# Split activations that begin 28 bytes into their SBUF slots: a one-layer decoder step on one core

## The chip, the core and the metric

The kernel runs on one core of one Trainium2 chip. The metric is the device time of one execution in microseconds, the median of several runs. Lower is better.

## What is computed

One inference step of a one-layer decoder, in float32, for 256 prompt tokens and 8 x 4 sample tokens (288 in all) at a model width of 2,048. Cut to what matters:

```python
mod = silu(c) @ w_ada + b_ada                       # 2048 -> 6 x 2048
h = rms(x, g_mix) * (1 + sc_m) + sh_m
b_gate, c_gate, hc, u, v, ga, gb = split(h @ w_in)  # 2048 -> 9216
ya = b_gate * causal_conv3(c_gate * hc)
yb = gelu(u) * (spatial_mix(rms(gelu(v))) + b_sg)
merged = sigmoid(ga) * (ya @ w_pa) + sigmoid(gb) * (yb @ w_pb)
x = x + gt_m * (merged @ w_out)
h2 = rms(x, g_ffn) * (1 + sc_f) + sh_f
gate, up = split(h2 @ w_ffn_in)                     # 2048 -> 2 x 5632
x = x + gt_f * ((silu(gate) * up) @ w_ffn_out)
return rms(x, g_final), conv state, v rows
```

Every weight is used once, for all 288 tokens.

## The kernel before

Activations stand transposed: 128 features on the partitions, the 288 tokens along the free dimension. A tile of 128 features x 288 tokens of float32 is one **slot** of the pool `slots`, which has 92 of them (`SLOTS`, line 24). Each slot is padded to 298 words (`TU = T + 10`), because some tiles carry ten extra columns beside the 288. In the built program the slots lie 1,216 bytes apart in each partition and every one begins on a multiple of 32 bytes (32 past a multiple of 64).

Float32 products are made from three matmuls on the faster type `float32r`. An operand `a` is split into `hi`, its rounding to `float32r` (a cast on ScalarE), and `lo = a - hi` (a subtraction on VectorE). `triple` (line 227) then issues `hi·hi` (L229), `hi·lo` with the activation's low part (L232) and `lo·hi` with the weight's low part (L234). All of them accumulate in one PSUM bank. The activation is the moving operand, 288 columns wide; the weight tile, 128 x 128, is loaded before each matmul.

Weights are streamed from HBM in blocks (`raw`), ahead of their use through a ring of 7 buffers, and split in pieces of four tiles into the rings `hi` and `lo` (L453 on ScalarE, L459 or L248 on VectorE). These rings are in another pool than the slots. For each output tile of 128 features, `Blk.run` goes over the tiles of the contraction and calls `triple` for each. A sink then takes the result out of PSUM and does the pointwise work. The order of TensorE's work is written out by hand: the adaLN projection (`ada`, L393, on unsplit float32), the input projection, the two branches, the output projection, and the feed-forward in four quarters.

The split activations are made in these places: `split` (L299 to L304; for `ya`, `yb`, `mg` and `act`), `modulate` (hi at L316, lo at L326; for `h1` and `h2`) and `make_h1` (L645 and L651; for part of `h1`). All of them call `slot(F32R)` with 288 columns. Two kinds of split tiles are 298 wide: `xe` in `scaled_tile` (L675), which the first output tiles use, and `xg` (L939), which the first blocks of the feed-forward use. Slots of plain float32 hold partial sums and small tables; matmuls don't stream them as the moving operand of a split product.

Of the kernel before, what the change touches and what calls it, by code (L numbers as in the profile page):

```python
# [9 lines left out]
F32R = mybir.dt.float32r  # L10
# [4 lines left out]
P = 128  # L15
D = 2048
T = 288
TP = 256
TU = T + 10
# [2 lines left out]
NC = 9  # L22
DFF = 5632
SLOTS = 92
RAW = 7
LEAD = 12
LAG = 2
# [57 lines left out]
def decoder_kernel(tc, d):  # L85
# [3 lines left out]
    with ExitStack() as es:  # L89
        def pool(name, bufs=1, **kw):  # L90
            return es.enter_context(tc.tile_pool(name=name, bufs=bufs, **kw))

        pc = pool("const")
        pw = pool("wstream")
        pslot = pool("slots", SLOTS)
        ptmp = pool("tmp", 5)
# [5 lines left out]
def _body(tc, nc, d, pc, pw, pslot, ptmp, pps):  # L102
    ids = [0]

    def nm(s):
        ids[0] += 1
        return f"{s}_{ids[0]}"
# [2 lines left out]
        return pc.tile(shape, dt, tag=name, name=name)  # L110

    def slot(dt=F32, shape=(P, T)):
        return pslot.tile(list(shape), dt, tag="s", name=nm("s"), padded_shape=[P, TU])

    def tmp(n=T):
        return ptmp.tile([P, n], F32, tag="t", name=nm("t"), padded_shape=[P, TU])
# [182 lines left out]
    def split(a, n=T):  # L299
        hi = slot(F32R, (P, n))  # L300
        A.copy(hi, a)  # L301
        lo = slot(F32R, (P, n))
        V.tensor_tensor(lo, a, hi.bitcast(F32), ALU.subtract)  # L303
        return hi, lo  # L304

    def normed(kt, rb):
        t = slot()
        V.tensor_tensor(t, x[:, kt, :], rb, ALU.mult)
        return t
# [52 lines left out]
    class Ada(Step):  # L362
# [7 lines left out]
        def load(self):  # L370
            n = self.nk * 4 * self.w
            self.raw = pw.tile([P, n], F32, tag="raw", name=nm("raw"), bufs=RAW, padded_shape=[P, 2048])
            w = 1024 if self.nk == 8 else n
# [50 lines left out]
    class Blk(Step):  # L424
# [4 lines left out]
        def load(self, a0=0, a1=None):  # L429
            n = self.nk * self.nm * 128  # L430
            self.raw = self.raw or pw.tile([P, n], F32, tag="raw", name=nm("raw"), bufs=RAW, padded_shape=[P, 2048])
            for a in range(a0, a1 or n, self.cut or n):
# [145 lines left out]
    def squares1():  # L578
        qa, qb = (pw.tile([P, 2048], F32, tag="raw", name=nm("q"), bufs=RAW) for _ in range(2))
        for q in (qa, qb):  # L580
            G.memset(q[:, 7 * T : 7 * T + 1], 0.0)

        def part_of(q, o, n):
            return q[:, o * T : (o + n) * T].rearrange("p (k t) -> p k t", t=T)

        q1, q0, q2, q4 = part_of(qa, 0, 4), part_of(qa, 4, 2), part_of(qb, 0, 4), part_of(qb, 4, 2)

        def square(q, a, b):
            return lambda: A.activation(q, x[:, a:b, :], AF.Square)

        def add(o, q):
            return lambda: V.tensor_tensor(o, o, q, ALU.add)

        S["sq"] = q1[:, 0]
        return {
            ("wK", 0, 4): square(q0, 0, 2),
            ("wA", 0, 1): square(q1, 2, 6),
            ("wA", 0, 3): add(q1[:, 0:2], q0),
            ("wA", 0, 5): square(q2, 6, 10),
            ("wA", 0, 7): add(q1, q2),  # L600
            ("wA", 1, 1): square(q2, 10, 14),
            ("wA", 1, 3): add(q1, q2),
            ("wA", 1, 4): square(q4, 14, 16),
            ("wA", 1, 6): add(q1[:, 0:2], q1[:, 2:4]),
            ("wA", 2, 0): add(q1[:, 0:2], q4),
            ("wA", 2, 3): add(q1[:, 0], q1[:, 1]),
        }
# [405 lines left out]
    def finish():  # L1013
# [28 lines left out]
        def stored(i, cuts):  # L1042
            w, name = ((P, "o_ya"), (T - P, "o_yb"))[i]
            t0 = TB[halves[i][0]]
            for o, e in zip(cuts, cuts[1:]):
                st = pw.tile([P, (e - o) * w], F32, tag="raw", name=nm("st"), bufs=RAW, padded_shape=[P, 2048])
                v = st.rearrange("p (m t) -> p m t", t=w)
# [101 lines left out]

    AHEAD = RAW  # L1150
    n = len(steps)
# [167 lines left out]
```

## Time and profile before

| what | value |
|---|---|
| median of 3 runs | 1624.26 us (1624.0 to 1624.49) |
| profiled execution, its own time | 1624.22 us |
| span of the profiled execution, first to last instruction | 1622.4 us |
| mean granted TensorE clock | 0.998 |
| instructions in the span | 31,579 |
| read from HBM | 352.74 MB, 219 GB/s over the span |

How to read the lines that follow below. A line of a group of instructions gives the program line, the engine, the operation, `output<-inputs` by the program's names with their shape, and the count; then the busy time in us and the mean duration of one in ns; then the idle time of the engine just before these instructions in us and what ended most of it. PE is TensorE's matmul and PEld its weight load, which overlaps with PE; DVE is VectorE and ACT is ScalarE. Matmuls are pipelined: their durations overlap, and their ends are modelled, so a pace is read from starts or from counts. `s` is a tile in a slot, `hi` and `lo` are weight tiles, `pm` and `px` PSUM banks, `t` a temporary tile. A row for a stretch of time gives its ends and its length in us, the busy time of the engines PE, PEld, DVE, ACT and POOL in us with the number of instructions that touch it (or of PE alone, where only PE was asked for), the granted clock, the mean busy share of the DMA engines, and the GB/s they moved. A row of the timeline gives the start and the length in us, the engine, the line, the operation and how many were merged into the row.

### The profile page before, as it was taken

What the parts mean: (1) busy time and instruction counts of PE and PEld (TensorE: products, weight loads), DVE (VectorE), ACT (ScalarE), POOL (GpSimd) and SP (SyncE); (2) the same over time, 40 slices, a digit from 0 to 9 for tenths busy, and PEclk for the clock granted to TensorE, in tenths of its full rate; (3) what the DMA queues carried; (4) which work ended last, traced back from release to release, by engine and by line L of the source; (5) the groups of instructions that cost most, each with busy time, mean ns of one, the idle gap of its engine ahead of it and who ended that gap; (6) DMA issues with size and microseconds to landing.
All of it is one profiled execution on the core that took longest, in us unless ns stands there. A gap on an engine that the chain in (4) does not pass through costs nothing.

```text
span 1622.4 us, 31579 instructions
## 1 busy us (share of the span) xinstructions
PE 1611.5 (99%) x12641; PEld 1547.6 (95%) x12641; DVE 1017.0 (63%) x2194; ACT 737.3 (45%) x1360; POOL 21.2 (1%) x65
## 2 busy tenths in 40 slices
PE   9999999999999999999999999999999999999997
PEld 8998999899999999999999999999999999999997
DVE  6676788877755667667744555555555555555565
ACT  5533344643444434456643444444444444444454
POOL 0000000000000000011000000000000000000000
PEclk9999999999999999999999999999999999999999
DMA  9887866777778676654576556443564534645341
GB/s 376 324 319 287 312 237 212 273 279 295 288 281 337 260 271 227 236 176 157 193 304 251 217 177 208 159 172 110 169 224 156 173 117 161 226 157 172 109 162 59
DMA packets 59476, 357.88 MB, mean 221 GB/s; under 512 B 6720, under 2 KB 10176, under 8 KB 28608
## 3 DMA queue, kind: packets, MB, share of 16 engines
q1 hardware_dynamic: 59040, 355.73, 59.8%
q8 instruction: 99, 1.62, 0.4%
q14 instruction: 49, 0.40, 0.1%
q10 hardware_dynamic: 288, 0.13, 0.0%
HBM read 352.74 MB, written 3.09 MB: 219 GB/s over the span
## 4 chain that ended last, share of the span: by engine, by line
PE 98%; DMA 1%; DVE 0%; ACT 0%; DVEq 0%; issue 0%; ACTq 0%
PE pm L229 31%; PE pm L234 30%; PE pm L232 30%; PE ada L393 5%; DMA raw<-in_wK 1%; DMA raw<-in_w 0%; DVE st L1048 0%; DMA ct<-in_c 0%; PE px L232 0%; PE px L229 0%; PE px L234 0%; PE px L880 0%; PE px L879 0%; PE px L826 0%; PE px L203 0%; ACT hi L453 0%
## 5 line engine op out<-in xcount | busy, mean ns | idle before, releaser
L229 PE MATMUL pm<-s,hi 128*128 128x288 f32 (+1 forms) x3750 | 1109.1, 296 | 0.0
L232 PE MATMUL pm<-s,hi 128*128 128x288 f32 (+1 forms) x3750 | 1103.8, 294 | 0.0
L234 PE MATMUL pm<-s,lo 128*128 128x288 f32 (+1 forms) x3738 | 1102.2, 295 | 0.0
L453 ACT CAST hi<-raw 128x512 fp32r<-128x512 f32 (+1 forms) x963 | 587.2, 612 | 803.3 <-PE pm L232 762.6
L459 DVE TENSOR_TENSOR lo<-raw,hi 128x512 fp32r<-128x512 f32 (+1 forms) x849 | 578.7, 683 | 437.9 <-ACT hi L453 425.3
L229 PEld LDWEIGHTS pm<-s,hi 128*128 128x128 f32 x3750 | 705.7, 188 | 15.2 <-issue 13.0
L232 PEld LDWEIGHTS pm<-s,hi 128*128 128x128 f32 x3750 | 704.7, 188 | 0.0
L234 PEld LDWEIGHTS pm<-s,lo 128*128 128x128 f32 x3738 | 702.9, 188 | 0.0
L248 DVE TENSOR_TENSOR lo<-raw,hi 128x512 fp32r<-128x512 f32 x111 | 74.6, 675 | 29.6 <-ACT hi L453 28.9
L393 PE MATMUL ada<-raw,cs 128*32 128x512 f32 (+2 forms) x1152 | 88.3, 452 | 0.2 <-DMA raw<-in_a 0.2
L393 PEld LDWEIGHTS ada<-raw,cs 128*32 128x32 f32 x1152 | 30.9, 110 | 45.0 <-issue 41.1
L771 DVE TENSOR_TENSOR s<-pm,s 128x288 f32<-128x288 f32 x72 | 32.8, 456 | 19.9 <-PE pm L234 19.7
L301 ACT CAST s<-t 128x288 fp32r<-128x288 f32 (+1 forms) x76 | 32.9, 433 | 18.8 <-DVE t L803 12.4
L303 DVE TENSOR_TENSOR s<-t,s 128x288 fp32r<-128x288 f32 (+1 forms) x76 | 34.9, 459 | 6.5 <-ACT s L301 6.4
L343 DVE SCALAR_TENSOR_TENSOR x<-pm,mod,x 128x256 f32<-128x256 f32 x79 | 37.6, 475 | 0.0
L969 DVE SCALAR_TENSOR_TENSOR t<-t,pm 128x288 f32<-128x288 f32 x42 | 19.1, 454 | 20.9 <-PE pm L234 20.9
L763 DVE TENSOR_TENSOR s<-pm,s 128x288 f32<-128x288 f32 x48 | 21.8, 454 | 10.4 <-PE pm L234 9.5
L342 DVE TENSOR_TENSOR t<-pm,mod 128x32 f32<-128x32 f32 x79 | 15.2, 192 | 18.3 <-PE pm L234 18.2
L748 DVE SCALAR_TENSOR_TENSOR s<-pm,s 128x256 f32<-128x256 f32 x48 | 23.1, 480 | 4.1 <-PE pm L234 4.1
L754 DVE TENSOR_TENSOR s<-s,rb 128x288 f32<-128x288 f32 x48 | 21.5, 448 | 0.0
L171 ACT ACTIVATE t<-x 128x288 f32<-128x288 f32 x29 | 12.9, 445 | 17.4 <-DVE x L346 17.4
L176 DVE TENSOR_TENSOR acc<-acc,t 128x288 f32<-128x288 f32 x33 | 15.0, 455 | 8.2 <-ACT t L171 8.2
(164 smaller groups left out, 470.9 us busy)
## 6 DMA issues: line engine op xcount, KB each, us to landing
raw<-in_fi SPq DMA_DIRECT2D x84, 1024.0 KB, 4.8
raw<-in_a SPq DMA_DIRECT2D x64, 1024.0 KB, 7.9
raw<-in_f SPq DMA_DIRECT2D x64, 704.0 KB, 4.0
raw<-in_wD SPq DMA_DIRECT2D x34, 1024.0 KB, 5.4
raw<-in_aE SPq DMA_DIRECT2D x16, 1024.0 KB, 9.6
raw<-in_wo SPq DMA_DIRECT2D x16, 1024.0 KB, 6.0
raw<-in_wC SPq DMA_DIRECT2D x19, 768.0 KB, 4.3
raw<-in_pa SPq DMA_DIRECT2D x8, 1024.0 KB, 5.9
```

Source lines behind the costliest of these rows:

```text
L229: PE.matmul(out, wh, ah, start=first, stop=False)
L232: end_ = PE.matmul(out, wh, al, start=False, stop=turn and last)
L234: end_ = PE.matmul(out, wl, ah, start=False, stop=last)
L248: lows.pop(0)[1]()
L301: A.copy(hi, a)
L303: V.tensor_tensor(lo, a, hi.bitcast(F32), ALU.subtract)
L343: V.scalar_tensor_tensor(x[:, m, :TP], ps[:, :TP], mod[:, gt0 + m, 0:1], x[:, m, :TP], ALU.mult, ALU.add)
L393: PE.matmul(acc[32 * j : 32 * j + 32, :w], cs[:, kt, :], self.raw[:, o : o + w], start=kt == 0, stop=kt == 15, tile_position=(0, 32 * j), ...
L453: A.copy(hi, self.raw[:, s * 128 : e * 128])
L459: sub()
L748: V.scalar_tensor_tensor(t[:, :TP], ps[:, :TP], t[:, T : T + 1], t[:, :TP], ALU.add, ALU.add)
L771: V.tensor_tensor(a, ps[:, :T], a, ALU.add)
```

## The change

`slot` gets an offset. A slot asked for as `float32r` and no wider than 288 columns is made as a tile of 7 + 288 columns, of which the caller gets the part from the eighth column on: it begins 28 bytes into the slot. A slot of plain float32, or one of 298 columns, begins at its first byte, as before. The padded size, the number of slots, and every instruction's order and shape stay as they are. The lines behind move by three: L229, L232 and L234 become L232, L235 and L237.

```diff
 SLOTS = 92
+LEADIN = 7
 RAW = 7
...
     def slot(dt=F32, shape=(P, T)):
-        return pslot.tile(list(shape), dt, tag="s", name=nm("s"), padded_shape=[P, TU])
+        o = LEADIN if dt == F32R and shape[1] <= T else 0
+        t = pslot.tile([P, o + shape[1]], dt, tag="s", name=nm("s"), padded_shape=[P, TU])
+        return t[:, o:] if o else t
```

## The prediction

> **What bounds the kernel now.** I read the page's busy times first, then the chain of work that ended last, then the groups of instructions with shapes kept apart, and last the matmul starts one by one. The busy times and the chain:
>
> ```profile
> PE 1611.5 (99%) x12641; PEld 1547.6 (95%) x12641; DVE 1017.0 (63%) x2194; ACT 737.3 (45%) x1360; POOL 21.2 (1%) x65
> PE 98%; DMA 1%; DVE 0%; ACT 0%; DVEq 0%; issue 0%; ACTq 0%
> ```
>
> TensorE is busy for 99% of the span and is 98% of the chain. A busy PE is not yet a PE at its peak, so the question is how far apart its matmuls start. First, how many of them does the change touch? The groups, shapes kept apart:
>
> ```profile
> L229 PE MATMUL pm<-s,hi 128*128 128x288 f32 x3626 | 1071.5, 295 | 0.0
> L234 PE MATMUL pm<-s,lo 128*128 128x288 f32 x3626 | 1068.6, 295 | 0.0
> L232 PE MATMUL pm<-s,hi 128*128 128x288 f32 x3626 | 1066.5, 294 | 0.0
> L229 PEld LDWEIGHTS pm<-s,hi 128*128 128x128 f32 x3750 | 705.7, 188 | 15.2 <-issue 13.0 <-ACT t L353 0.8 <-ACT s L301 0.8
> ```
>
> The first three rows are the three products of a split matmul, 3 x 3,626 = 10,878 matmuls whose moving operand is one of the 288-wide split activations. The mean of 295 ns is the length of one from start to modelled end; they overlap, so it is not the pace. The last row shows that the engine hardly waits: 15.2 us before this line's weight loads in the whole span, 0.8 us of it for the activations' split (ACT s L301). The pace comes from stretches of time that hold nothing but such matmuls:
>
> ```profile
> 1000.00:1200.00 200.00, 200.00 (x1514) 200.00 (x1513) 109.30 (x205) 86.79 (x153) 0.00 (x0) 1.00 0.47 164
> 1200.00:1400.00 200.00, 200.00 (x1514) 200.00 (x1513) 108.93 (x204) 87.20 (x152) 0.00 (x0) 1.00 0.48 163
> 341.00:366.00 25.00, 25.00 (x192) 25.00 (x192) 18.61 (x48) 10.09 (x17) 0.00 (x0) 1.00 0.88 350
> 1210.00:1235.00 25.00, 25.00 (x191) 25.00 (x191) 13.20 (x22) 11.23 (x20) 0.00 (x0) 1.00 0.50 166
> ```
>
> The count in the first bracket is of matmuls that touch the stretch, about two more than start in it, so the pace is 200 us / 1,512 = 132.2 ns, in both long stretches. The clock granted is 1.00. The two short ones say that neighbours don't set this pace: with the DMA engines at 0.88 and VectorE busy 18.61 of 25 us there are 192 matmuls, at 0.50 and 13.20 us there are 191. So 10,878 x 132.2 ns = 1,438 us of the span goes at a pace that TensorE sets by itself. The change has to act on this number or on nothing.
>
> Is 132.2 ns what 288 columns must take? The last microseconds have bf16 matmuls of the same width, reading half the bytes:
>
> ```profile
> 1611.82 0.28 PE L576 MATMUL pm<-wb 128*128 128x288 bf16 x1
> ...
> 1612.32 0.65 PE L576 MATMUL pm<-wb 128*128 128x288 bf16 x4
> ```
>
> One lasts 0.28 us, four in a row 0.65, so they start (0.65 - 0.28) / 3 = 0.123 us apart: 0.427 ns a column. The split matmuls take 132.2 - 123 = 9.2 ns more each, 100 us over all of them. The trace does not say what those 9.2 ns are. They may lie in the reading of the moving operand, in the weight loads (188 ns here), or in the handing over from one matmul to the next.
>
> One more row bears on it: the matmuls of the 298-wide tiles, which the change leaves where they are. Two runs of starts on TensorE, first 288 wide, then 298 wide, each with the first and the last row; 43 intervals lie between the first two, 28 between the last two:
>
> ```profile
> 1000.29 0.29 PE L229 MATMUL pm<-s,hi 128*128 128x288 f32 x1
> ...
> 1005.98 0.29 PE L232 MATMUL pm<-s,hi 128*128 128x288 f32 x1
> ```
>
> ```profile
> 767.02 0.30 PE L229 MATMUL pm<-s,hi 128*128 128x298 f32 x1
> ...
> 770.88 0.30 PE L232 MATMUL pm<-s,hi 128*128 128x298 f32 x1
> ```
>
> That is 5.69 / 43 = 132.3 ns and 3.86 / 28 = 137.9 ns. Ten more columns cost 5.6 ns, where ten columns at 0.427 ns would cost 4.3. A tile of 298 elements does not end on a multiple of four elements, one of 288 does. If the operand is fetched in pieces of four elements (16 bytes), 288 columns are 72 pieces and 298 are 75: 132.3 / 72 x 75 = 137.8 ns, which is what stands there. In pieces of eight it would be 36 and 38, or 139.7 ns. This is thin, since another stretch of 298-wide matmuls goes faster:
>
> ```profile
> 22.00:41.00 19.00, 19.00 (x142) 1.00 0.99 394
> ```
>
> Here it is 19 us / 140 = 135.7 ns, only 3.5 ns over 132.2, and that fits no pieces at all.
>
> **The change part by part.** It moves no instruction: on every engine the same instructions stand in the same order, with the same waits, buffers and sizes. A slot keeps its 298 words of room, and 7 + 288 = 295 fit. Only the start address in the operands of split activations changes, on three engines.
>
> *ScalarE and VectorE.* They write and read the moved tiles when they split an activation:
>
> ```profile
> L301 ACT CAST s<-t 128x288 fp32r<-128x288 f32 x60 | 26.0, 433 | 18.8 <-DVE t L803 12.4 <-DVE t L897 4.4 <-DMA raw<-in_pa 1.4
> L303 DVE TENSOR_TENSOR s<-t,s 128x288 fp32r<-128x288 f32 x60 | 27.1, 452 | 1.1 <-ACT s L301 1.0
> L797 DVE SCALAR_TENSOR_TENSOR t<-t,cp,t 128x255 f32<-128x255 f32 x8 | 3.8, 476 | 0.0
> L343 DVE SCALAR_TENSOR_TENSOR x<-pm,mod,x 128x256 f32<-128x256 f32 x79 | 37.6, 475 | 0.0
> ```
>
> L797 writes its tile from the second element on and takes 476 ns for 255 elements; L343 starts at the first and takes 475 for 256. So an odd start costs VectorE a nanosecond or two, perhaps nothing. No row has ScalarE at an odd start; bounds are a gain of nothing and, by the same rows, a few ns on a cast of 433. The program splits 108 activations (16 of h1, 16 of h2, 8 of ya, 8 of yb, 16 of mg, 44 of act). Even 20 ns on each cast and each subtraction would be 108 x 40 ns = 4 us, spread over engines that are 45% and 63% busy, while TensorE waits 0.8 us for their results in the row of L229's weight loads above. What hides them is the matmul work queued ahead; if that cover went, at most those 4 us would show. I take 0.
>
> *TensorE.* 10,878 matmuls read their moving operand from 28 bytes past a multiple of 32 in place of from a multiple of 32. No row of the trace has a split matmul at such a start, so the cost is bounded from both sides. Below: if the start takes away what lies between the bf16 pace and this one, -9.2 ns each, -100 us. Above: one more piece for each read. From 28 bytes in, the first four-element piece gives one element and the last one three: 73 pieces in place of 72, so 132.2 / 72 = 1.84 ns more, x 10,878 = +20.0 us. In pieces of eight elements it is 37 for 36: 3.67 ns, +39.9 us. And zero, if reading is ahead of need. I take the four-element piece, since the row it is nearest to is that of the 298-wide tiles, the only one here in which a read does not fill its pieces, and there the steady stretch shows it at 137.9 ns. At the bf16 price of a column a piece is 4 x 0.427 = 1.7 ns, and 18.6 us; I take 1.75 ns, between the two: +19.0 us.
>
> [...]
>
> *The sum.* The profiled execution took 1624.22 us, 1.82 of it around the span of 1622.4; the median of the runs is 1624.26, so the two agree. 1624.3 + 0 (ScalarE, VectorE) + 19.0 (TensorE) = 1643 us.
>
> **The rivals.** *Nothing happens* (chance 0.22). For it: the pace does not move with DMA or VectorE load (192 against 191 matmuls in 25 us), so reading may not be the tight part, and the 298-wide stretch at 135.7 ns shows no pieces. Then the edit costs nothing and 1624.3 us stays. A chance in this that the change does not do what it says is small: the 298-wide split tiles keep their start, but the three groups of 3,626 do move.
>
> *The start sets how the moving read meets the weight read, and the new start is better* (0.36, faster). Place: every matmul of L229, L232 and L234, beside the weight load of the next one. Both now start on a multiple of 32 bytes and run at the same time; if they get in each other's way piece by piece, moving one of them 28 bytes changes which pieces meet. For it: 9.2 ns per matmul are unaccounted for, they are missing in the bf16 matmuls, whose reads are half as heavy, and no load outside TensorE explains them. Against it: nothing in the trace shows that a start matters, and a gain has first to pay for the added piece. It decides from 1.75 ns on. Price: a third of the 9.2 ns net, 3.1 ns x 10,878 = -33 us, 1591 us; half is 1574, all of it 1524. [...]
>
> *The piece is larger than I take it* (0.05, slower by more): eight elements give 1664 us. A read that breaks into two for every pair of elements would near double the pace, over 2,500 us; I leave that outside, at about one in a hundred, within this chance.
>
> **How the numbers follow.** The forecast, one more piece of 16 bytes for each read, has a chance of 0.37: 1643 us, by itself 1634 (half a piece, where the rest hides behind the previous matmul) to 1650. Slower in all is 0.37 + 0.05 = 0.42, the same 0.22, faster 0.36. Within 0.2% is 3.2 us either way, about what a measurement of this kernel can tell from no change; spread over 10,878 matmuls that is 0.3 ns each, so any effect of a start on reading would pass it. The range reaches up to the eight-element piece, 1666, and down through the faster case to a little under half of its full gain, 1568. That leaves about 0.1 of larger gains below and a few hundredths above. Cases of both signs hold most of the chance, and the forecast is the likeliest of them by little.
>
> **What would show it.** In the changed kernel's profile: the three groups again 3,626 times each; in 200 us from 1000 on, about 1,494 matmuls touched in place of 1,514 (200 / 0.13395 + 2); 298-wide matmuls as before; L301 and L303 within 5 ns of 433 and 452; no new wait of weight loads on ACT s. The forecast is wrong if that count is 1,512 or more. If it is above 1,520 the reads met each other and now do so less; if it stays at 1,514, starts don't matter; at 1,475 the piece is eight elements. If the count stays and the span changes, my view that only the pace can move is wrong, and the cause lies in a wait.

## The result and the profile after

The changed kernel takes 1615.18 us (median of 4 runs, 1614.98 to 1615.49) against 1624.26 before: a ratio of 0.9944, with a 95% interval from 0.9927 to 0.9962. It is faster by 9.1 us, where the forecast was slower by 19. The profiled execution has a span of 1613.3 us, 9.1 less than before.

The page's busy times of the changed kernel, and its chain of work by engine:

```profile
PE 1602.6 (99%) x12641; PEld 1538.5 (95%) x12641; DVE 1016.6 (63%) x2194; ACT 736.0 (46%) x1360; POOL 21.5 (1%) x65
PE 98%; DMA 1%; DVE 0%; ACT 0%; DVEq 0%; issue 0%; ACTq 0%
```

TensorE's busy time fell by 8.9 us, from 1611.5, for the same number of instructions; that is nearly the whole 9.1. The chain is as it was. The groups that answer to those shown of before, with shapes kept apart, first TensorE's, then the split's:

```profile
L232 PE MATMUL pm<-s,hi 128*128 128x288 f32 x3626 | 1064.6, 294 | 0.0
L235 PE MATMUL pm<-s,hi 128*128 128x288 f32 x3626 | 1060.7, 293 | 0.0
L237 PE MATMUL pm<-s,lo 128*128 128x288 f32 x3626 | 1062.3, 293 | 0.0
L232 PE MATMUL pm<-s,hi 128*128 128x298 f32 x124 | 37.6, 303 | 0.0
L232 PEld LDWEIGHTS pm<-s,hi 128*128 128x128 f32 x3750 | 706.0, 188 | 15.3 <-issue 13.0 <-ACT t L356 0.8 <-ACT s L304 0.8
L304 ACT CAST s<-t 128x288 fp32r<-128x288 f32 x60 | 26.0, 433 | 18.9 <-DVE t L806 12.5 <-DVE t L900 4.4 <-DMA raw<-in_pa 1.4
L306 DVE TENSOR_TENSOR s<-t,s 128x288 fp32r<-128x288 f32 x60 | 27.2, 453 | 1.1 <-ACT s L304 1.0
```

The three groups of 3,626 each lost 6 to 7 us. The fourth row is of the 298-wide matmuls, which were not moved: 303 ns, as before. The weight loads wait as long as they did (15.3 us against 15.2), and the splitting takes what it took: the cast 433 ns, the subtraction 453 in place of 452. So no wait went and no other engine matters; the matmuls that read a moved tile start closer together. The stretches of time for the same places as before:

```profile
1000.00:1200.00 200.00, 200.00 (x1526) 200.00 (x1525) 110.78 (x211) 87.30 (x153) 0.00 (x0) 1.00 0.49 168
1200.00:1400.00 200.00, 200.00 (x1526) 200.00 (x1525) 109.87 (x206) 87.28 (x153) 0.00 (x0) 1.00 0.49 166
341.00:366.00 25.00, 25.00 (x193) 25.00 (x191) 19.75 (x50) 10.49 (x19) 0.00 (x0) 1.00 0.82 322
```

There are 1,526 matmuls in 200 us where there were 1,514: 200 / 1,524 = 131.2 ns in place of 132.3. In the early stretch there is one more in 25 us. Over the whole span 9.1 us / 10,878 = 0.84 ns a matmul.

### The profile page after: what moved, and what is told of

The parts are those of the page before. It is cut to its first block, busy times and chain, and to the rows that moved or that the text cites. A ratio compares the mean times of both kernels' runs of the same rounds, so it can differ in the third digit from the quotient of the medians.

```text
span 1613.3 us, 31579 instructions
## 1 busy us (share of the span) xinstructions
PE 1602.6 (99%) x12641; PEld 1538.5 (95%) x12641; DVE 1016.6 (63%) x2194; ACT 736.0 (46%) x1360; POOL 21.5 (1%) x65
## 4 chain that ended last, share of the span: by engine, by line
PE 98%; DMA 1%; DVE 0%; ACT 0%; DVEq 0%; issue 0%; ACTq 0%
PE pm L232 31%; PE pm L237 30%; PE pm L235 30%; PE ada L396 5%; DMA raw<-in_wK 1%; DMA raw<-in_w 0%; DVE st L1051 0%; DMA ct<-in_c 0%; PE px L235 0%; PE px L232 0%; PE px L237 0%; PE px L883 0%; PE px L882 0%; PE px L829 0%; PE px L206 0%; ACT hi L456 0%
## 5 line engine op out<-in xcount | busy, mean ns | idle before, releaser
L232 PE MATMUL pm<-s,hi 128*128 128x288 f32 (+1 forms) x3750 | 1102.2, 294 | 0.0
L235 PE MATMUL pm<-s,hi 128*128 128x288 f32 (+1 forms) x3750 | 1097.9, 293 | 0.0
L237 PE MATMUL pm<-s,lo 128*128 128x288 f32 (+1 forms) x3738 | 1095.8, 293 | 0.0
L232 PEld LDWEIGHTS pm<-s,hi 128*128 128x128 f32 x3750 | 706.0, 188 | 15.3 <-issue 13.0
L235 PEld LDWEIGHTS pm<-s,hi 128*128 128x128 f32 x3750 | 705.7, 188 | 0.0
L237 PEld LDWEIGHTS pm<-s,lo 128*128 128x128 f32 x3738 | 703.1, 188 | 0.0
```

Of the source, the lines that this page charges most:

```text
L232: PE.matmul(out, wh, ah, start=first, stop=False)
L235: end_ = PE.matmul(out, wh, al, start=False, stop=turn and last)
L237: end_ = PE.matmul(out, wl, ah, start=False, stop=last)
```

## The experiments

What had to be told apart: does the moving read's own start count, or how far it lies from the start of the weight read, or merely that the tiles lie elsewhere? And how can a read that by the forecast touches one more piece of 16 bytes be faster? The edit of the first run, against the changed kernel; the second has 8 in place of 1:

```diff
-LEADIN = 7
+LEADIN = 1
```

The third and fourth move the weights' hi tile, and lo likewise; the third has `LEADIN = 0` beside it, the fourth keeps 7:

```diff
-                hi = pw.tile([P, w], F32R, tag="hi", name=nm("hi"), bufs=SPB, padded_shape=[P, SEG * 128])
+                hi = pw.tile([P, 7 + w], F32R, tag="hi", name=nm("hi"), bufs=SPB, padded_shape=[P, SEG * 128 + 16])[:, 7:]
```

**A start of 4 bytes.** 

> The split activations begin 4 bytes into their slots (the changed kernel: 28). Theory O (the moving read's own start, off a multiple of 32 bytes by any amount, saves 0.84 ns a matmul): as the changed kernel, 1613 to 1617 us, about 1,526 matmuls touched in the 200 us from 1000 on. Theory R (only the distance from the start of the moving read to that of the weight read counts): a distance of 4 bytes is neither 0 nor 28, so anything between 1610 and 1624 us. Theory L (28 is good because the first piece of 32 bytes gives a single element, and the next piece is asked for at once): with 4 bytes seven elements come from the first piece, and the time is that of the kernel before, 1624 us, 1,514 matmuls.

Measured: 1662.05 us, a ratio of 1.0231 to the kernel before (1.0216 to 1.0246), slower by 38 us. Its long stretch:

```profile
1000.00:1200.00 200.00, 200.00 (x1478) 200.00 (x1477) 106.19 (x197) 85.04 (x149) 0.00 (x0) 1.00 0.47 158
```

48 matmuls fewer than in the changed kernel: 200 / 1,476 = 135.5 ns. None of the three theories had a time above 1624. An odd start as such is not good: against a start of 0, one of 4 bytes cost 38 us and one of 28 saved 9.1.

**A start of 32 bytes.** 

> The split activations begin 32 bytes into their slots, again on a multiple of 32 and now of 64 bytes too. Theories O, R and L, with pieces of 32 bytes, all expect the kernel before: 1624 us, 1,514 matmuls in the 200 us from 1000 on. If the piece is 64 bytes, theory O expects nothing new to learn from the start (it would be on a multiple of 64) and a time that may differ from both by up to the 9 us measured. A time of 1615 us would say that any move of the activations does it, whatever the start within a piece, so that the cause is the slot's place and not its alignment.

Measured: 1630.45 us, ratio 1.0036 (1.0023 to 1.0049). Its long stretch:

```profile
1000.00:1200.00 200.00, 200.00 (x1511) 200.00 (x1510) 108.42 (x203) 86.61 (x151) 0.00 (x0) 1.00 0.48 164
```

That is 200 / 1,509 = 132.5 ns, and a time 6 us above the kernel before and 15 above the changed one, so moving the tiles is not what helps. The 6 us are clear of noise, and nothing that follows explains them.

**The weights moved, not the activations.** 

> The activations begin at their first byte again; the split weights begin 28 bytes into their ring buffers. Theory R: the distance between the two reads is 28 bytes the other way, the two no longer start together, and the time falls as in the changed kernel, 1613 to 1618 us. Theories O and L: the moving read is as before, 1624 us and 1,514 matmuls in the 200 us from 1000 on.

**Both moved.** 

> Activations and split weights both begin 28 bytes in, so that the two reads of TensorE again start at the same place within a piece. Theory R: the gain is lost, 1624 us and 1,514 matmuls in the 200 us from 1000 on. Theories O and L: the gain stays, 1613 to 1617 us and 1,526 matmuls.

Measured: 1632.96 us with the weights alone (1.0052, from 1.0037 to 1.0067), 1611.49 us with both (0.9921, from 0.9904 to 0.9937). The long stretch of each, weights alone first:

```profile
1000.00:1200.00 200.00, 200.00 (x1503) 200.00 (x1503) 108.25 (x202) 86.15 (x150) 0.00 (x0) 1.00 0.48 162
```

```profile
1000.00:1200.00 200.00, 200.00 (x1531) 200.00 (x1530) 110.98 (x212) 87.95 (x153) 0.00 (x0) 1.00 0.49 167
```

Theory R falls on both: with the two reads apart by moving the weights, 1,503 matmuls and not 1,526; with the two reads again at the same place, 1,531 and not 1,514. The gain goes with the activations' own start. But moving the weights is not without effect: with them alone it cost 8.5 us, which no theory had expected, and with both it brought 3.7 us over the changed kernel. The 8.5 us are clear of noise. The intervals of the two ratios behind the 3.7 us overlap, though the count of matmuls went the same way, from 1,526 to 1,531. The edit also lays the weights' ring buffers 64 bytes further apart; a later run tells what that does.

**All starts.** The next two runs give each kind of split activation a start of its own, so that one run holds several. The edit of the first; the second has 11, 11, 12, 13 and (14, 15, 3, 12) in the same places:

```diff
-LEADIN = 7
+LEADIN = {'h1': 2, 'y': 2, 'mg': 3, 'h2': 4, 'act': (5, 6, 9, 10)}
...
-    def slot(dt=F32, shape=(P, T)):
-        o = LEADIN if dt == F32R and shape[1] <= T else 0
+    def slot(dt=F32, shape=(P, T), o=0):
+        o = o if dt == F32R and shape[1] <= T else 0
...
```

The rest of the edit hands each caller's start to `slot` and pads a slot to 304 words, the 1,216 bytes that it took before. Each of the two ran once, in 1638.91 and 1633.23 us.

> Each kind of split activation gets a start of its own, in elements of 4 bytes: h1, ya and yb 2, mg 3, h2 4, act 5, 6, 9 and 10 in its four quarters; the slots stay where they are. The pace of a stretch then belongs to one start. Known from whole kernels: start 0 132.2 ns, 1 135.7, 7 131.35, 8 132.7. Theory P16 (the operand is fetched in pieces of 16 bytes, and what counts is how full the last piece is): a period of four, so 5 and 9 at 135.7, 3 at 131.4, 4 at 132.5, 2, 6 and 10 near 133.5. Theory P32 (pieces of 32 bytes): a period of eight, falling evenly from 135.7 at start 1 to 131.35 at 7, so 2 at 135.0, 3 at 134.2, 4 at 133.5, 5 at 132.8, 6 at 132.1, 9 at 135.7, 10 at 135.0. Theory M (it is not the start but some other mark of the tiles): every stretch within 0.5 ns of the kernel before, 131.5 to 132.8.

> The same with other starts: h1, ya and yb 11, mg 12, h2 13, act 14, 15, 3 and 12 in its four quarters. Theory P16: 11, 15 and 3 at 131.4 ns, 12 at 132.5, 13 at 135.7, 14 near 133.5. Theory P32: 11 at 134.2, 12 at 133.5, 13 at 132.8, 14 at 132.1, 15 at 131.35, 3 at 134.2. Theory M: every stretch at 131.5 to 132.8.

TensorE's count of matmuls in stretches that hold one start each. The first run, with starts 3, 5, 4, 6, 9, 10 and 2 in that order of rows:

```profile
670.00:730.00 60.00, 60.00 (x462) 1.00 0.50 168
940.00:1000.00 60.00, 60.00 (x444) 1.00 0.57 197
1010.00:1070.00 60.00, 60.00 (x454) 1.00 0.48 163
1150.00:1210.00 60.00, 60.00 (x450) 1.00 0.58 193
1360.00:1420.00 60.00, 60.00 (x448) 1.00 0.55 186
1560.00:1620.00 60.00, 60.00 (x452) 1.00 0.29 97
346.00:382.00 36.00, 36.00 (x270) 1.00 0.75 283
```

The second run, with starts 12, 14, 13, 15, 3, 12 and 11:

```profile
660.00:720.00 60.00, 60.00 (x456) 1.00 0.50 170
930.00:990.00 60.00, 60.00 (x450) 1.00 0.57 191
1010.00:1070.00 60.00, 60.00 (x446) 1.00 0.46 158
1143.00:1203.00 60.00, 60.00 (x460) 1.00 0.57 196
1355.00:1415.00 60.00, 60.00 (x460) 1.00 0.59 198
1555.00:1615.00 60.00, 60.00 (x457) 1.00 0.29 97
341.00:377.00 36.00, 36.00 (x276) 1.00 0.76 290
```

With two taken off each count, and the whole kernels beside them, the pace in ns by the start in elements (of 4 bytes):

| elements past a multiple of four | starts | pace, ns | elements in the first piece, in the last |
|---|---|---|---|
| 0 | 0, 4, 8, 12 | 132.3, 132.7, 132.5, 131.9 to 132.2 | 4, 4 |
| 1 | 1, 5, 9, 13 | 135.5, 135.7, 134.5, 135.1 | 3, 1 |
| 2 | 2, 6, 10, 14 | 134.3, 133.9, 133.3, 133.9 | 2, 2 |
| 3 | 3, 7, 11, 15 | 130.4 to 131.0, 131.2, 131.4, 131.0 | 1, 3 |

The period is four elements, 16 bytes, and theory P16 had these paces within 1.2 ns; P32 and M are out (start 3 would be at 134.2 or 132). P16 gave the last piece as the reason; the next run is about that. Starts of one row scatter by up to 1.2 ns, so finer rules can't be read from stretches.

**First piece or last piece.** At 288 columns the two go together. A kernel with narrower matmuls parts them:

```diff
-                    triple(
-                        ps[:, : self.width], self.parts[j * self.nk + k], self.rhs(self.k0 + k), k == 0, k == self.nk - 1
-                    )
+                    w = self.cols() if k else self.width
+                    a = tuple(t[:, :w] for t in self.rhs(self.k0 + k))
+                    triple(ps[:, :w], self.parts[j * self.nk + k], a, k == 0, k == self.nk - 1)
```

> This kernel leaves out the last tokens' products in part of the feed-forward: from the second contraction tile on, the matmuls are narrower than 288 columns (quarters of the down projection 286 each, act starting 0, 1, 2 and 3 elements into its slots; in the up projection h2 starts 3 in and the widths are 288, 286, 284, 282 by quarter). So the elements in the first and in the last piece of 16 bytes, tied together at 288 columns, come apart: at 286 the four starts give (first, last) = (4, 2), (3, 3), (2, 4), (1, 1). Two columns less are 0.8 ns less, 131.4 ns for whole pieces. Theory LAST (a last piece that is hardly filled is dear, a short first one is not): 133.0, 130.5, 131.4 and 134.8 ns in the four down quarters; with h2, 131.1 at 288 (1, 3), 134.8 at 286 (1, 1), 129.4 at 284 (1, 3), 133.1 at 282 (1, 1). Theory FIRST (the first piece decides; one element in it is good, three are dear): 131.4, 134.8, 133.0 and 130.5; with h2 131.1, 130.3, 129.4 and 128.6. Theory START (the address alone, whatever first and last hold): the sweeps' paces less 0.8, so 131.4, 134.8, 133.0, 130.3: with FIRST here, since the width doesn't enter.

The four quarters of the down projection (286 columns, starts 0, 1, 2, 3), then the second to fourth quarters of the up projection (start 3; 286, 284, 282 columns):

```profile
930.00:990.00 60.00, 60.00 (x460) 1.00 0.59 201
1135.00:1195.00 60.00, 60.00 (x452) 1.00 0.57 186
1342.00:1402.00 60.00, 60.00 (x456) 1.00 0.57 188
1537.00:1597.00 60.00, 60.00 (x461) 1.00 0.29 97
1010.00:1070.00 60.00, 60.00 (x460) 1.00 0.50 170
1210.00:1270.00 60.00, 60.00 (x467) 1.00 0.51 175
1420.00:1480.00 60.00, 60.00 (x469) 1.00 0.49 165
```

That is 131.0, 133.3, 132.2 and 130.7 ns (the first contraction tile of each output tile, one matmul in eleven here and one in sixteen in the up projection, is still 288 wide); FIRST and START expected 131.4, 134.8, 133.0 and 130.5 (130.3), LAST 133.0, 130.5, 131.4 and 134.8. The order is that of the start, and LAST is wrong by 2 to 4 ns in every quarter but the third. FIRST and START miss the second quarter by 1.5 ns. At start 3 the widths give 131.0, 129.0 and 128.5 ns: 284 columns are 2.0 ns cheaper than 286, and 282 another 0.5. A last piece with one element (286, 282) so costs a nanosecond at most over an even slope, not the 3 ns of LAST.

The end may count for something. At one start, two columns less save most where the read also touches one piece less: 2.2 ns at start 1 (135.5 to 133.3), 1.7 at start 2 (133.9 to 132.2), 2.0 at start 3 from 286 to 284. Where the number of pieces stays, they save 1.3 ns (start 0), 0.3 (start 3, 288 to 286) and 0.5 (284 to 282). The means differ by 1.3 ns. With a scatter of 1.2 ns between starts of one row that is a hint, and no run was made for it. Start and first piece stay tied together here: which of the two names is the better one, no run says.

**The weights' start, with the activations at 12 bytes.**

```diff
+WLEAD = {'': 0, 'fi': (0, 1, 2, 3), 'f0': 4, 'f1': 5, 'f2': 6, 'f3': 7, 'wo': 8}
...
+            q = WLEAD["fi"][(self.idx + 4) // 22] if self.name == "fi" else WLEAD.get(self.name, WLEAD[""])
...
-                hi = pw.tile([P, w], F32R, tag="hi", name=nm("hi"), bufs=SPB, padded_shape=[P, SEG * 128])
+                hi = pw.tile([P, q + w], F32R, tag="hi", name=nm("hi"), bufs=SPB, padded_shape=[P, SEG * 128 + 16])[:, q:]
```

> All 288-wide split activations begin 3 elements (12 bytes) in, and the split weights begin at a start of their own by stream: up projection 0, 1, 2, 3 elements in by quarter, down projection 4, 5, 6, 7, output projection 8, all else 0. Theory W0 (the weight load has room, and its start is worth 0.4 ns at most): every stretch at 130.7 to 131.3 ns. Theory W4 (the weight read follows the same rule of 16-byte pieces as the moving read): starts 1 and 5 dearer by 2 ns or more, 3 and 7 at 130.6 to 131.0, 2 and 6 between, 0 and 4 at 131.1.

Weights starting 1, 2 and 3 elements in (up projection, second to fourth quarter):

```profile
1010.00:1070.00 60.00, 60.00 (x461) 1.00 0.51 172
1210.00:1270.00 60.00, 60.00 (x458) 1.00 0.48 161
1410.00:1470.00 60.00, 60.00 (x458) 1.00 0.48 167
```

That is 130.7, 131.6 and 131.6 ns. The down quarters at 4, 5, 6 and 7 elements have 459, 460, 458 and 459 in 60 us (from 925, 1130, 1338 and 1540 us on), the output projection at 8 has 459 (from 670). Start 1 is the cheapest and not 2 ns dearer, so W4 is out; the spread of a nanosecond is a little more than W0 gave. The whole execution, the only one, took 1615.02 us.

Two more things can be read from this run. With the activations fixed at 12 bytes, the distance between the two reads takes all four values within 16 bytes, and the pace stays within a nanosecond, from 130.7 to 131.6 ns; so it is not the distance that makes the 4 ns between the activations' starts. And the matmuls whose weights stay at 0 start 131.2 ns apart, as the same 4,771 matmuls do with `LEADIN = 3` and the rings unpadded (a later run), by the starts in the two traces. The wider spacing of the rings alone therefore does nothing that shows.

**hi and lo apart.** The split takes a start for each:

```diff
+LEADIN = {'h1': (7, 0), 'y': (7, 0), 'mg': (0, 1), 'h2': (1, 0), 'act': ((0, 3), (3, 0), (1, 3), (3, 1))}
...
-        hi = slot(F32R, (P, n))
+        hi = slot(F32R, (P, n), o and o[0])
...
```

> hi and lo of an activation get different starts (hi, lo, in elements): mg (0, 1), h2 (1, 0), act (0, 3), (3, 0), (1, 3), (3, 1) by quarter, h1, ya and yb (7, 0). Of the three matmuls of a product two read hi and one lo. Theory OWN (each read pays for its own start, with the paces of whole kernels and sweeps: 132.2 for 0, 135.6 for 1, 131.0 for 3 or 7): 133.3 ns for mg, 134.5 for h2, then 131.8, 131.4, 134.1 and 132.5 in the down quarters, 131.4 to 131.6 for h1. Theory CHAIN (what counts is how a read joins on to the one before it, and with equal starts they always joined alike): mixed starts then pay for something else, and at least one stretch is off these numbers by 1 ns or more.

The four quarters of the down projection, then a quarter of the up projection (h2) and the output projection (mg):

```profile
930.00:990.00 60.00, 60.00 (x458) 1.00 0.60 202
1140.00:1200.00 60.00, 60.00 (x460) 1.00 0.59 198
1350.00:1410.00 60.00, 60.00 (x448) 1.00 0.55 185
1550.00:1610.00 60.00, 60.00 (x454) 1.00 0.29 97
1010.00:1070.00 60.00, 60.00 (x451) 1.00 0.49 169
660.00:720.00 60.00, 60.00 (x452) 1.00 0.50 167
```

131.6, 131.0, 134.5, 132.7, 133.6 and 133.3 ns, against 131.8, 131.4, 134.1, 132.5, 134.5 and 133.3 expected by OWN. The largest miss is 0.9 ns, at h2; the others are within 0.4, and no stretch is off by the 1 ns that CHAIN asked for. So in these six stretches the mean pace of a product is, within 0.9 ns, what the starts of its three reads give one by one. Single matmuls don't divide so neatly. In h2, by the starts in the trace, the two that read hi at start 1 are followed after 135.1 and 133.1 ns, where 135.6 is the pace of start 1, and the one that reads lo at start 0 after 133.6, where 132.2 is that of start 0. Some share of how one read joins on to the next is not excluded.

**Faster versions.** The first moves all split activations to 12 bytes, the 298-wide ones too, and the weights to 28; the second is the changed kernel with `LEADIN = 3`; the third is the second with the weights at 12 bytes as well.

> All split activations, the 298-wide ones too, begin 3 elements (12 bytes) into their slots, and the split weights 28 bytes into their buffers. Theory START (a moving read is best 12 bytes past a multiple of 16, wherever that lies; weights at 28 bytes are worth another 0.4 ns): 1610 to 1613 us, the 450 matmuls of the 298-wide tiles each 1 ns shorter, which is 0.4 us and can't be told. Theory 28 (28 bytes is special, 12 is not): 1615 us or more.

> The changed kernel with 12 bytes in place of 28, weights where they are. Theory START (a multiple of 16 plus 12 is what counts): as the changed kernel, 1614 to 1617 us. If 12 and 28 differ (pieces of 32 bytes count a little too): 1617 to 1620 us.

> Split activations and split weights both begin 12 bytes in. If the weights' 0.36 ns in the run with both at 28 came from equal starts of the two reads: 1610 to 1613 us again. If it came from the weights' own start at 28: 1614 to 1617 us, as without it.

Measured: 1614.06 us (0.9937, from 0.9920 to 0.9953), 1612.30 us (0.9926, from 0.9911 to 0.9941) and 1616.65 us (0.9953, from 0.9937 to 0.9970). The first misses what START gave by a microsecond and isn't as slow as theory 28 gave. The second beats its expectation by 2 us: 12 bytes are no worse than 28. The third rules out equal starts as the reason for the 3.7 us that weights at 28 bytes brought, since at 12 they bring nothing. The weights' own start at 28 is no sure reason either: the first kernel has it too and is no faster than the second. So all five kernels whose 288-wide activations lie 12 past a multiple of 16 throughout, with one start for all weights, come out between 1611.5 and 1616.7 us, and those at 0 past a multiple at 1624 to 1633. The fastest is the one with both at 28 bytes, 1611.49 us, 3.7 us below the changed kernel; `LEADIN = 3` alone is 0.8 us above it. The intervals of the five ratios, some 2.7 us either way, overlap or touch, so their order among themselves is not settled.

## Why the prediction was wrong

*What bounds the kernel* was right: the gain is TensorE's pace, 8.9 of 9.1 us, with the waits unchanged. *ScalarE and VectorE at 0* was right to a nanosecond, 433 and 453 ns. *Nothing happens* is out: the count went from 1,514 to 1,526, and the ratio's interval lies below 1.

*The step that failed* is "one more piece for each read", that is "73 pieces in place of 72, so 132.2 / 72 = 1.84 ns more, x 10,878 = +20.0 us". That TensorE fetches its operand in pieces was an assumption, and no run shows a piece; what the runs show is that the paces repeat every four elements, 16 bytes, the size that the forecast took. The price and its sign were wrong: the changed start came out 0.84 ns a matmul cheaper. Starts of 1, 2 and 3 elements past a piece would all touch 73 pieces, and cost +2.8, +1.5 and -1.3 ns against whole pieces (means of the table's rows: 135.2, 133.9 and 131.1 against 132.4). So the number of pieces alone does not set the time. The pace goes with where within 16 bytes the read starts, and among these three the pace falls with each element the first piece lacks. At 4 bytes the forecast's sign would have been right, by luck, and its size half of what was measured.

*The row it rested on* was that of the 298-wide tiles, which start on a whole piece and end in a half-filled one. It speaks of the end of a read, the change moved its start. At one start the narrow matmuls do hint at a price for one more piece, about 1.3 ns against the forecast's 1.84; the start, with 4.1 ns between 131.1 and 135.2, outweighs it. The stretch at 135.7 ns, which fitted no pieces, was the warning.

*The rival that ended faster* had the sign, and the sign came from the same clue, 9.2 ns per matmul that the bf16 matmuls don't have. Its mechanism, in the form that the distance between the two reads decides, fell with the weights moved alone, with both moved and with the weights' starts varied. So its sign was luck, and the prediction's mark for it, a count above 1,520, was met (1,526) without its cause. Its size was out as well: 0.84 ns of the 9.2, where a third was the price. The remaining 8 ns are still unexplained. (The prediction's counts of 1,494 and 1,475 come out at 1,495 and 1,474 by its own sums; nothing hangs on it.)

*What stays open.* Why a start at 12 bytes past a multiple of 16 is better than one at 0 was not shown, only that it is (131.1 ns against 132.4). Nor is it settled why a start of 32 bytes costs 6 us more than one of 0, or what the weights' start does: with activations at 0, weights at 28 lose 8.5 us; with activations at 28, they gain 3.7; with activations at 12, weights at 12 lose 4.4 and at 28, with the 298-wide tiles moved as well, 1.8. The sign changes with the activations' start, so an effect of the two reads on each other, other than by their distance, stays possible; no run tells whether the 8.5 us come from the weight read by itself or from the two together.

## What to carry to other kernels

When one engine's pace is the whole span, the start address of what it streams can be tried as a setting like any other: here the four starts within 16 bytes lie 4 ns apart on 132, and trying them takes one constant. One run can hold many settings, if each stretch of the program gets its own and the matmuls of a stretch are counted. And a row stands as evidence for the thing that differs in it; here the 298-wide read, which ends in a part-filled piece and had 137.9 ns, said little on one that starts in one, which has 131.2.

## What the runs showed of the hardware

- 288-wide float32r matmuls at a granted clock of 1.00 start 131.1, 132.4, 133.9 or 135.2 ns apart when the moving operand starts 12, 0, 8 or 4 bytes past a multiple of 16 (means of four starts each, which scatter by up to 1.2 ns). The cast and the subtraction that write such tiles took 433 and 453 ns at a start of 28 bytes, 433 and 452 at 0.
- With different starts for hi and lo, the mean pace of the three matmuls of a split product is that of their own starts, within 0.9 ns.
- Moving the stationary operands' start changed the time of the whole kernel by -3.7 to +8.5 us, with no rule found.
- Unsplit float32 matmuls of 128 columns (L879, L880 and L884 of the kernel before, from 551.03 us on) started 0.111 us apart (0.89 us from the first to the ninth); the float32r matmuls of 288 columns started 0.132 us apart in the same kernel.
